# A hybrid trunk kernel: the head by halves, one pool per k tile for u and y, two xbc tiles in one loop, ten conditioning products earlier

## The chip, the cores and the metric

The kernel runs on one core of one Trainium2 chip. Its five engines each take their instructions in order from a queue of their own: TensorE (PE, matrix products, with weight loads shown as PEld), VectorE (DVE), ScalarE (ACT), GpSimd (POOL) and SyncE (SP, here only a queue of transfers). The metric is device time in microseconds (us), lower is better; the median of several executions counts.

## The reference, cut to what matters

One layer over a sequence of 1024 positions with 1024 channels, all in 32-bit floats:

```python
mod = (silu(c) @ w_ada + b_ada).reshape(6, 1024)      # shift1, scale1, gate1, shift2, scale2, gate2
u = rms_norm(x, ln1) * (1.0 + scale1) + shift1
proj = u @ w_in                                       # 1024 -> 11296 columns
gl, cb, cc, cx, z, xbc, dt = split(proj)              # 2048, 3 x 1024, 2048, 4096, 32
y_conv = cb * causal_conv3(cc * cx)
p_conv = y_conv @ w_conv_out
xs, bs, cs = split(silu(causal_conv4(xbc) + bias))    # 2048, 8 x 128, 8 x 128
y = ssd_scan(xs * dt, dt * a, bs, cs) + d_skip * xs   # state-space recurrence, 8 groups
y = group_rms(y * silu(z)) * ssm_norm_w
p_ssm = y @ w_ssm_out
x = x + gate1 * ((sigmoid(gl_a) * p_conv + sigmoid(gl_b) * p_ssm) @ w_o)
u2 = rms_norm(x, ln2) * (1.0 + scale2) + shift2
x = x + gate2 * (square(relu(u2 @ w_up)) @ w_down)
out = rms_norm(x)
```

## The kernel before, in words

Everything is held transposed: channels on the 128 partitions, time along the free axis, in two halves of 512 columns (`hs`). A product of a weight tile with an activation is made with three matmuls, since both are split in a high part and a low part of a faster 32-bit format: high times high, high times low, low times high (`mm3`, L119). One output tile of 128 columns of `w_in` (a *plain* product, `proj`, L126) over 8 k tiles and 2 halves is 48 matmuls of 512 columns; two output tiles are 96. `strassen_pair` (L146) makes two output tiles with 7 block products of 12 matmuls, 84, at the price of sums and differences of weights and results on DVE. It needs combinations of u (`tops_of`, L138, the lists `X`), which are made after the head. Weight tiles come on SP's queue (`wraw`, three buffers), ACT rounds the high part (`whi`), DVE subtracts for the low part (`wlo`), or, in `load_w_acc` (L100), a transfer on POOL's queue adds it up.

The order of work within an engine is chosen by a planner when the program is built: it simulates the engines with a cost model and takes instructions by program order and readiness. `tc.issue_after` pins an instruction behind another. On the chip each engine then follows that fixed order, and waits on semaphores.

*Head* (L267 to L372). `c` is loaded as one row, spread over the partitions by two matmuls, and turned into silu(c) (`cb`). x comes in 16 loads (8 k tiles, 2 halves). ACT squares each, DVE adds the squares, matmuls with a vector of ones sum over partitions (L321), `rsqrt_eps` makes the root for both halves at once, and the diagonal `sdg` times ones spreads it over the partitions (L331). Then a loop over the k tiles j (L342): two conditioning products (`gemv`, L302, a multiply and sum of a 128 x 1024 tile with `cb` on DVE) give the scale and shift columns of this tile; for both halves DVE scales x, ACT adds the shift and rounds (`uh`), DVE makes the residue (`ul`); then PE adds this k tile into four output tiles, f = 0 to 3, both halves, in all eight PSUM banks. The results go through tanh to scratch memory (`gl_d`).

*After the head*: tiles f = 4, 5 are made plain while DVE and ACT make the combinations of u (L380 to L391); the 32 dt columns are projected (L395 to L415, memory in pool `p0d`); then pool `pe1`, which takes over the same bytes, serves the Strassen pairs: f = 6 to 15 (L457), eight pairs for z (L470), twelve for the short convolution (L491). `dt_chain` (L432) is a long run of small DVE operations, placed at f = 8. The other 32 conditioning products (`gemvs`, L423) are placed three per pair from f = 10 on; each loads its tile on POOL's queue into one single buffer, `wv`.

*State-space part* (L547 to L697): for each of eight groups, four xbc tiles are made plain (`xbc_tile`, L560: product, copy to a padded row `raw`, four-tap convolution starting with two ACT operations on PSUM, silu), and the eight chunks of the group before run among them (`ssd_group`). After the last group's tiles, the pool `u` is released (L698), and a pool `yy` on the same side takes over its bytes for the split tiles of y (L700 to L707), which the next products read (`wco`, L713 on; then `wso`, L728 on).

*Rest*, not touched: `w_o`, the second norm, the up and down products and the final norm.

Of the kernel before, what the change touches and what calls it, by code (L numbers as in the profile page):

```python
# [34 lines left out]
NPAR = DSK + 16  # L35


def hybrid_trunk(tc, xT, par, hrows, crow, wada1, wada2, win, wdt, wco, wso, wo, wup, wdt_, wdn, out):
# [20 lines left out]
    prm = cp.tile([P, NPAR], F32, name="prm")  # L59
# [3 lines left out]
    onec = cp.tile([P, P], F32R, name="onec")  # L63
    mcol = cp.tile([P, 48], F32, name="mcol")
    s1c = cp.tile([P, 8], F32, name="s1c")
    s2c = cp.tile([P, 8], F32, name="s2c")
    g1c = cp.tile([P, 8], F32, name="g1c")
    cp.tile([P, 24], F32, name="lpad")
# [193 lines left out]
    p0x = tc.alloc_tile_pool(name="p0x", bufs=1)  # L262
    p0 = tc.alloc_tile_pool(name="p0", bufs=2)
# [7 lines left out]
    crw = glp.tile([1, T], F32, name="crw", tag="glt")  # L271
    sp.dma_start(crw, crow)
    sp.dma_start(prm, par)
    for h in (0, 1):
        ps = mm.tile([P, H], F32, name="mm")
        pe.matmul(ps, lhsT=ones[0:1, :], rhs=crw[:, hs[h]], start=True, stop=True)
        act.activation(ct[:, hs[h]], ps, AF.Tanh, scale=0.5)
        stt(cb[:, hs[h]], ct[:, hs[h]], 1.0, ps, ALU.add, ALU.mult)
# [26 lines left out]
    def warm(n, x_):  # L305
        for _ in range(n):
            pe.matmul(wps, lhsT=ones, rhs=x_, start=True, stop=True)

    warm(4, xt[0][0])
    st = ps0.tile([P, H], F32, name="st")  # L310
    for h in (0, 1):
        acc = None
        for k in range(KT):
            sq = p0.tile([P, H], F32, name="ssq" if k else "sacc", bufs=4 if k else 2)
            act.activation(sq, xt[k][h], AF.Square)
            if k:
                tt(acc, acc, sq, ALU.add)
            else:
                acc = sq
        for j in range(4):  # L320
            pe.matmul(st[:, 4 * h + j:4 * h + j + 1], lhsT=acc[:, j * P:j * P + P], rhs=ones[:, 0:1],  # L321
                      start=h == j == 0, stop=True, skip_group_check=True)
    warm(2, acc)
    r = rsqrt_eps(p0, st[:, 0:8], 1.0 / T, [P, 8], "nst")
    rbs = []
    for h in (0, 1):
        dg = p0.tile([P, 4, P], F32, name="sdg", bufs=1)
        rdy = tt(dg, ident.unsqueeze(1).broadcast_to([P, 4, P]),
                 r[:, 4 * h:4 * h + 4].unsqueeze(2).broadcast_to([P, 4, P]), ALU.mult)
        ps = ps0.tile([P, H], F32, name="st")  # L330
        pe.matmul(ps, lhsT=ones, rhs=dg.rearrange("p j t -> p (j t)"), start=True, stop=True)  # L331
        rb = p0x.tile([P, H], F32, name=f"rb{h}")
        rbc = act.copy(rb, ps)
        rbs.append(rb)

    ws = []
    sps = [[None, None] for _ in range(4)]
    for h in (0, 1):
        for f in range(4):
            pl, nm = (mm, "mm") if f < 2 else (ps0, ("sx", "st")[h])  # L340
            sps[f][h] = pl.tile([P, H], F32, name=nm)
    for j in range(KT):  # L342
        if j > 1:
            load_ada(j)
        if j in (0, 1):
            with tc.issue_after(rdy.ins), (tc.issue_after(rbc.ins) if j else contextlib.nullcontext()):
                for f in range(2):
                    ws.append(load_w(win[2 * j + f], raws[2 * j + f]))
        with tc.issue_after(rdy.ins) if j else contextlib.nullcontext():
            gemv(wa[j, 1], 8 + j)  # L350
            gemv(wa[j, 0], j)
        stt(s1c[:, j:j + 1], mcol[:, 8 + j:9 + j], 1.0, prm[:, LN1 + j:LN1 + j + 1], ALU.add, ALU.mult)
        for h in (0, 1):
            x_ = xt[j][h]
            stt(x_, x_, s1c[:, j:j + 1], rbs[h], ALU.mult, ALU.mult)
            rdy = shift_split(uh[j][h], ul[j][h], x_, mcol[:, j:j + 1])
        if j == 0:
            continue
        for jj in ((0, 1) if j == 1 else (j,)):
            for h in (0, 1):  # L360
                for f in range(4):
                    mm3([sps[f][h]], ws[f][0][:, jj * P:jj * P + P], ws[f][1][:, jj * P:jj * P + P],
                        [uh[jj][h]], [ul[jj][h]], jj == 0, jj == KT - 1)

    def gl_evac(f, ps):
        t = glp.tile([P, T], F32, name="glt")
        for h in (0, 1):
            act.activation(t[:, hs[h]], ps[h], AF.Tanh, scale=0.5)
        act.dma_start(gl_d[f], t)

    for f in range(4):
        gl_evac(f, sps[f])  # L372
# [43 lines left out]

    p0d.release()
# [39 lines left out]
    for f in range(6, 16, 2):  # L457
        ts_ = [glp.tile([P, T], F32, name="glt") for _ in (0, 1)]

        def gl_ev(i, h, src):  # L460
            act.activation(ts_[i][:, hs[h]], src, AF.Tanh, scale=0.5)

        if f == 8:
            dt_chain()
        elif f > 8:
            gemvs(3)
        strassen_pair(pe1, win[f], win[f + 1], X, gl_ev)
        for i in (0, 1):
            act.dma_start(gl_d[f + i], ts_[i])
    for g in range(NG):  # L470
        ts_ = [glp.tile([P, T], F32, name="glt") for _ in (0, 1)]

        def z_ev(i, h, src):
            t = ts_[i][:, hs[h]]
            act.activation(t, src, AF.Tanh, scale=0.5)
            stt(t, t, 1.0, src, ALU.add, ALU.mult)

        gemvs(3)
        strassen_pair(pe1, win[gtile(g) + 4], win[gtile(g) + 5], X, z_ev)
        for i in (0, 1):  # L480
            act.dma_start(z_d[2 * g + i], ts_[i])
# [73 lines left out]
    padded = [p2t.tile([P, T + 3], F32, name=f"raw{i}", bufs=1) for i in (0, 1)]  # L555
# [4 lines left out]
    def xbc_tile(win_i, ci, dst):  # L560
        ps = proj(load_w_acc(win[win_i]), uh, ul)
# [4 lines left out]
        for h in (0, 1):  # L566
            act.activation(a[:, hs[h]], ps[h], AF.Identity, bias=hb[:, ci:ci + 1], scale=hw[:, 4 * ci + 3:4 * ci + 4])  # L567
        for j in (2, 1, 0):
            stt(a, raw[:, j:j + T], hw[:, 4 * ci + j:4 * ci + j + 1], a, ALU.mult, ALU.add)
        act.activation(dst, a, AF.Tanh)  # L570
        stt(dst, dst, 1.0, a, ALU.add, ALU.mult)

    def proj_group(g):
# [7 lines left out]
        xbc_tile(b + 2, 16 + g, bf)  # L581
        xbc_tile(b + 3, 24 + g, cf)
# [145 lines left out]
    for b in range(4):  # L728
        yh, yl = [], []
        for k in range(4):  # L730
# [7 lines left out]
            ys = yy.tile([P, 2, T], F32R, name="ys")  # L738
# [49 lines left out]
    yy.release()  # L788
# [282 lines left out]
```

## Time and profile before

| | |
|---|---|
| runs | 2106.76, 2107.31, 2111.0 us; median 2107.31 |
| profiled execution | 2108.83 us, its span 2107.1 us |
| PE busy | 2070.9 us (98%), 9704 matmul records |
| DVE, ACT, POOL busy | 1482.6 (70%), 962.8 (46%), 177.4 (8%) |
| mean granted TensorE clock | 0.990 |

A busy PE counts overlapping matmuls: one that shows 390 ns is followed by the next after about 0.226 us. A few matmul records are missing. In the rows below "L..." is a line of the kernel before; after "<-" in square brackets stands what ended the idle time of the engine ahead of an instruction.

### The profile page before, as it was taken

The numbers are of one execution on the slowest core, as the hardware profiler recorded it, in microseconds if no ns is written. First come the engines' busy times: TensorE is split into PE (matmuls) and PEld (weight loads), VectorE is DVE, ScalarE is ACT, GpSimd is POOL, SyncE is SP. The second block draws the span as 40 slices with busy tenths as digits, with TensorE's granted clock in tenths as the row PEclk, the third lists the DMA queues.
The fourth block names the chain that finished last, engine by engine and source line by source line (L and its number), as shares of the span: only waits on it lengthen the run. The fifth ranks groups of instructions, "written<-read, shape, count | busy, mean of one in ns | idle before, by whom it ended". The sixth has DMA issues, their size and how long they took to land.

```text
span 2107.1 us, 26132 instructions
## 1 busy us (share of the span) xinstructions
PE 2070.9 (98%) x9704; PEld 1689.8 (80%) x9704; DVE 1482.6 (70%) x2312; ACT 962.8 (46%) x1600; POOL 177.4 (8%) x244
## 2 busy tenths in 40 slices
PE   7999999999999999999999999999999999999997
PEld 4778878888888888887877788888888888888887
DVE  7866788676637778878796848745866665668675
ACT  4433333232246768676564531234544454544432
POOL 0001000000000000000000000012000001232213
PEclk8999999999999999999999999999999999999998
DMA  8226554222265455555366686553144347988932
GB/s 306 79 96 204 188 183 169 80 70 72 78 200 112 122 123 136 140 142 142 93 212 213 212 277 200 166 191 123 61 165 165 151 156 261 309 240 252 281 79 80
DMA packets 138224, 344.09 MB, mean 163 GB/s; under 512 B 12993, under 2 KB 48193, under 8 KB 136562
## 3 DMA queue, kind: packets, MB, share of 16 engines
q1 hardware_dynamic: 98978, 202.76, 30.2%
q0 software_dynamic: 26848, 103.82, 17.3%
q10 hardware_dynamic: 12272, 35.85, 4.3%
q8 instruction: 76, 1.25, 0.2%
q14 instruction: 50, 0.41, 0.1%
HBM read 269.83 MB, written 72.55 MB: 162 GB/s over the span
## 4 chain that ended last, share of the span: by engine, by line
PE 86%; issue 7%; DVE 4%; DMA 2%; POOL 1%; ACT 1%; SPq 0%; DVEq 0%; POOLq 0%; ACTq 0%
PE mm L155 26%; PE mm L124 14%; PE mm L122 14%; PE mm L121 14%; PE mm L965 11%; PE B L615 2%; PE B L620 2%; PE C L637 1%; DMA wv<-in_wada 1%; DVE wada L302 1%; PE A L592 1%; POOL wv L426 1%; DMA x<-in_xT 1%; DVE ul L46 1%; DVE x L46 0%
## 5 line engine op out<-in xcount | busy, mean ns | idle before, releaser
L155 PE MATMUL mm<-t,whi 128*128 128x512 f32 x1136 | 349.8, 390 | 1.6 <-DVE cq L43 1.6
L155 PEld LDWEIGHTS mm<-t,whi 128*128 128x128 f32 x1136 | 212.8, 188 | 47.9 <-DVE cq L43 4.0
L121 PE MATMUL mm<-uh,whi 128*128 128x512 f32 x576 | 228.0, 400 | 3.7 <-ACT uh L114 3.2
L122 PE MATMUL mm<-ul,whi 128*128 128x512 f32 x576 | 229.7, 399 | 0.0
L155 PE MATMUL mm<-t,wlo 128*128 128x512 f32 x568 | 220.4, 389 | 0.0
L965 PE MATMUL mm<-op,whi 128*128 128x512 f32 x672 | 206.9, 389 | 0.1
L124 PE MATMUL mm<-uh,wlo 128*128 128x512 f32 x576 | 185.3, 396 | 1.9 <-DVE wlo L43 1.9
L43 DVE TENSOR_TENSOR wlo<-s,whi 128x1024 fp32r<-128x1024 f32 (+1 forms) x126 | 126.5, 1015 | 66.3 <-ACT whi L160 65.4
L43 DVE TENSOR_TENSOR wlo<-wraw,whi 128x1024 fp32r<-128x1024 f32 (+1 forms) x135 | 144.1, 1068 | 15.3 <-ACT whi L95 8.9
L121 PE MATMUL mm<-ys,whi 128*128 128x512 f32 x384 | 149.3, 396 | 3.7 <-ACT ys L110 3.7
L122 PE MATMUL mm<-ys,whi 128*128 128x512 f32 x384 | 149.7, 396 | 1.1 <-DVE ys L43 1.1
L46 DVE SCALAR_TENSOR_TENSOR cacc<-raw,hw,cacc 128x1024 f32<-128x1024 f32 x96 | 122.7, 1278 | 38.5 <-ACT cacc L567 37.9
L965 PEld LDWEIGHTS mm<-op,whi 128*128 128x128 f32 x672 | 126.0, 188 | 26.7 <-issue 0.5
L160 ACT CAST whi<-wraw 128x1024 fp32r<-128x1024 f32 x78 | 65.3, 837 | 161.5 <-PE mm L155 140.9
L155 PE MATMUL mm<-s,whi 128*128 128x512 f32 x448 | 138.4, 389 | 0.7 <-ACT cu L178 0.7
L609 ACT ACTIVATE seg<-acb,acum 128x128 f32<-128x128 f32 x256 | 81.9, 394 | 110.4 <-PE B L615 104.6
L121 PEld LDWEIGHTS mm<-uh,whi 128*128 128x128 f32 x576 | 108.4, 189 | 28.3 <-ACT uh L114 5.3
L965 PE MATMUL mm<-op,wlo 128*128 128x512 f32 x336 | 130.7, 389 | 0.0
L95 ACT CAST whi<-wraw 128x1024 fp32r<-128x1024 f32 x57 | 59.8, 1052 | 152.8 <-PE mm L122 117.6
L124 PEld LDWEIGHTS mm<-uh,wlo 128*128 128x128 f32 x576 | 108.0, 189 | 24.2 <-DVE wlo L43 2.3
L122 PEld LDWEIGHTS mm<-ul,whi 128*128 128x128 f32 x576 | 109.0, 189 | 21.6 <-issue 0.5
L160 ACT CAST whi<-s 128x1024 fp32r<-128x1024 f32 x78 | 81.8, 1050 | 96.2 <-PE mm L155 95.2
(277 smaller groups left out, 4417.4 us busy)
## 6 DMA issues: line engine op xcount, KB each, us to landing
wraw<-in_win SPq DMA_DIRECT2D x87, 512.0 KB
dr<-in_wdt_ SPq DMA_DIRECT2D x108, 256.0 KB
op_d<-hp POOLq DMA_DIRECT2D x12, 1792.0 KB, 6.2
hr<-op_d POOLq DMA_DIRECT2D x42, 512.0 KB, 5.7
wv<-in_wada POOLq DMA_DIRECT2D x32, 512.0 KB, 3.8
wlo<-in_win POOLq DMA_DIRECT2D x32, 512.0 KB, 7.7
acb<-ac_d SPq DMA_DIRECT2D x64, 256.0 KB
wraw<-in_wup SPq DMA_DIRECT2D x32, 512.0 KB
```

What stands on the lines that cost most here:

```text
L43: return eng.tensor_tensor(out=o, in0=a, in1=b, op=op)
L46: return dve.scalar_tensor_tensor(out=o, in0=a, scalar=s, in1=b, op0=op0, op1=op1)
L95: act.copy(hi, raw)
L121: pe.matmul(o, lhsT=wh, rhs=h_, start=start, stop=False)
L122: pe.matmul(o, lhsT=wh, rhs=l_, start=False, stop=False)
L124: last_mm[0] = pe.matmul(o, lhsT=wl, rhs=h_, start=False, stop=stop)
L155: last_mm[0] = pe.matmul(o, lhsT=l_[:, s_], rhs=r_, start=first and k == j == 0, stop=k == 3 and j == 2, skip_group_check=True)
L160: act.copy(hi, src)
L609: act.activation(seg[:, r, :], acb[:, r, :], AF.Relu, bias=acum[:, c, hd:hd + 1], scale=-1.0)
L615: pe.matmul(Bk[o:o + 64, P * (r // 2):P * (r // 2) + P], lhsT=xd[:, r, :], rhs=seg[:, r, :], start=True, stop=True, skip_group_check=True)
L620: pe.matmul(Bk[:, 256 + P * q:256 + P * q + P], lhsT=state[:, 2 * q:2 * q + 2, :].rearrange("p r k -> p (r k)"), rhs=cf[:, cs], start=True ...
L965: pe.matmul(o, lhsT=l_[:, c_], rhs=t[:, r_, k, :], start=first and k == j == 0, stop=k == 3 and j == 2, skip_group_check=True)
```

## The change

1. **Head by halves.** Only the first half of x is loaded ahead of the weights; its squares, sums, root and spread are made alone. The loop over k tiles then makes only the first half of u, and PE adds it into eight output tiles, f = 0 to 7, each joined as soon as its weights are split. The second half's squares are put into steps 3 to 6, its root into step 7; after the loop the second half of u is made, and f = 4 to 7 and then 0 to 3 get it. So f = 4, 5 move into the head, and f = 6, 7, a Strassen pair before, become plain tiles there. The order on PE, ACT, DVE and SP is pinned, instruction by instruction, to the order written.
2. **First scale column on PE.** `wadak`, a block of `w_ada` laid out for PE, and `c` as columns (`CCOL` in `par`) give the scale of k tile 0 by eight one-column matmuls; the product on DVE for it goes.
3. **Weights in the head.** Tiles 0 to 2 come on SP's queue, 3 to 7 on POOL's; the low parts of 6 and 7 by an accumulating transfer. Conditioning tiles have four buffers, not eight.
4. **Ten conditioning products** are placed at the dt projection, in a pool `p0g` with three buffers between `p0d` and `pe1`; three each stay at f = 12 and 14, two each at the eight z pairs. `dt_chain` moves from f = 8 to f = 10.
5. **Start of the convolution**: one ACT operation of 1024 columns on `raw` instead of two of 512 on PSUM, in all xbc tiles; `raw` is padded to T + 32.
6. **Last two xbc tiles** (B and C of group 7): the k loops of both are interleaved.
7. **One pool per k tile** for u (`u0` to `u7`) and per tile for y (`yy0` to `yy7`).

The core of the diff (left out: pool names and releases, the moved definitions, host arrays):

```diff
+    for k in range(KT):
+        up = tc.alloc_tile_pool(name=f"u{k}", bufs=1, side="right")
+        for n, u_ in (("uh", uh), ("ul", ul)):
+            u_.append([up.tile([P, H], F32R, name=f"{n}{k}{h}") for h in (0, 1)])
...
+    def load_f(f):
+        raws.append(wp.tile([P, T], F32, name="wraw", bufs=3))
+        (sp if f < 3 else pool).dma_start(raws[f], win[f])
...
+    def low_by_dma(f):
+        act.mul(wls[f], raws[f], -1.0)
+        pool.dma_start(wls[f], win[f], accum_op=ALU.add)
...
+    load_x(0)
+    sp.dma_start(wk, wadak)
+    sp.dma_start(wa[0, 0], wada1[0, :, 0])
+    for f in range(3):
+        load_f(f)
+    load_ada(1)
+    load_x(1)
+    load_ada(2)
...
+    sums(0)
+    first_col()
+    high(0)
+    high(1)
+    dg = root(0)
+    stt(mcol[:, 8:9], cps[:, 0:1], 0.5, prm[:, BADA + 8:BADA + 9], ALU.mult, ALU.add)
+    scale_of(0)
+    ps = spread(dg)
+    warm(8)
+    gemv(wa[0, 0], 0)
+    scaled(0, 0, ps)
+    low(0)
+    shift_hi(0, 0)
+    keep_rb(ps)
+    high(2)
+    load_f(3)
+    low(1)
+    load_f(4)
+    for j in range(1, KT):
+        scale_col(j)
+        shift_lo(j - 1, 0)
+        if j == 1:
+            for i in (0, 1, 2):
+                part((0,), (0, 1), 0, (i,))
+            part((0,), (2,), 0, (0, 1))
+        scaled(j, 0)
+        gemv(wa[j, 0], j)
+        if j == 1:
+            load_ada(3)
+            low(2)
+            part((0,), (2,), 0, (2,))
+            load_f(5)
+        if j > 2:
+            for k in {3: (0, 1, 2), 4: (3, 4), 5: (5, 6), 6: (7,), 7: ()}[j]:
+                square(1, k)
+        shift_hi(j, 0)
...
+        if j == 3:
+            load_ada(5)
+            part((2,), range(4), 0)
+            part((2,), (4,), 0, (0, 1))
+            low(4)
+            part((0, 1, 2), (4,), 0, (2,))
+            part((0, 1, 2), (5,), 0, (0, 1))
+            load_f(7)
...
+        if j == 7:
+            dg = root(1)
+            part((6,), range(7), 0)
+            keep_rb(spread(dg))
+    shift_lo(7, 0)
+    part((7,), range(7), 0)
+    part(range(KT), (7,), 0)
+    scaled(0, 1)
     for j in range(KT):
...
+        shift_hi(j, 1)
+        if j < KT - 1:
+            scaled(j + 1, 1)
+        rdy = shift_lo(j, 1)
+        if j < 4:
+            gl_half(2 * j, 0)
+        part((j,), range(4, 8), 1)
+    for f in (0, 2):
+        for f_ in (f, f + 1):
+            part(range(KT), (f_,), 1)
...
-    for f in (4, 5):
-        gl_evac(f, proj(ws[f - 4], uh, ul))
+    def gemvs(n, pl, bufs=1):
+        for _, i in zip(range(n), gem):
+            w_ = pl.tile([P, T + 32], F32, name="wv", bufs=bufs)[:, 0:T]
+            pool.dma_start(w_, wada2[i])
+            gemv(w_, 16 + i)
...
+    p0g = tc.alloc_tile_pool(name="p0g", bufs=1, reuse_waits="tile")
+    gemvs(10, p0g, 3)
...
-    for f in range(6, 16, 2):
+    for f in range(8, 16, 2):
...
-        if f == 8:
+        if f == 10:
             dt_chain()
-        elif f > 8:
-            gemvs(3)
+        elif f > 10:
+            gemvs(3, pe1)
...
-        gemvs(3)
+        gemvs(2, pe1)
...
-        for h in (0, 1):
-            act.activation(a[:, hs[h]], ps[h], AF.Identity, bias=hb[:, ci:ci + 1], scale=hw[:, 4 * ci + 3:4 * ci + 4])
+        act.activation(a, raw[:, 3:3 + T], AF.Identity, bias=hb[:, ci:ci + 1], scale=hw[:, 4 * ci + 3:4 * ci + 4])
...
+        ws = [load_w_acc(win[b + i]) for i in (2, 3)]
+        ps = [[mm.tile([P, H], F32, name="mm") for _ in hs] for _ in ws]
+        for i, k in [(0, k) for k in range(4)] + [(i, k + 4 - 4 * i) for k in range(4) for i in (0, 1)] + [(1, k) for k in range(4, KT)]:
+            c_ = slice(k * P, k * P + P)
+            mm3(ps[i], ws[i][0][:, c_], ws[i][1][:, c_], uh[k], ul[k], k == 0, k == KT - 1)
+            if (i, k) == (0, KT - 1):
+                xbc_evac(ps[0], 16 + g, bf)
+        xbc_evac(ps[1], 24 + g, cf)
...
-    yy = tc.alloc_tile_pool(name="yy", bufs=8, side="right", reuse_waits="tile")
+    yys = [tc.alloc_tile_pool(name=f"yy{f}", bufs=1, side="right", reuse_waits="tile") for f in range(8)]
```

`part(js, fs, h, kinds)` issues, for k tiles `js` and output tiles `fs` of half `h`, the matmuls of the kinds 0 (high times high), 1 (high times low part of u) and 2 (low part of the weight times high).

More of the change, by code (lines that the diff above doesn't have):

```diff
@@ L57, in hybrid_trunk @@
     mm = tc.alloc_tile_pool(name="mm", bufs=4, space=PSUM)
-    prm = cp.tile([P, NPAR], F32, name="prm")
+    s1c, s2c, g1c, cc = [cp.tile([P, 8], F32, name=n) for n in ("s1c", "s2c", "g1c", "cc")]
     ident = cp.tile([P, P], F32, name="ident")
@@ L63, in hybrid_trunk @@
     onec = cp.tile([P, P], F32R, name="onec")
+    prm = cp.tile([P, NPAR], F32, name="prm")
     mcol = cp.tile([P, 48], F32, name="mcol")
[L65 to L68, printed above, removed]
+    ccol = cp.tile([P, 8], F32, name="ccol")
     dcs = cp2.tile([P, 64], F32, name="dc")
@@ new lines, in hybrid_trunk, with first_col, square @@
+    wk = p0w.tile([P, T], F32, name="wk", tag="whx")
+    sp.dma_start(wk, wadak)
+    wa[0, 0] = p0.tile([P, T], F32, name="wada", bufs=4)
+    sp.dma_start(wa[0, 0], wada1[0, :, 0])
[4 more added lines that the diff above has]
+    load_ada(2)
+    def first_col():
+        for k in range(KT):
+            pe.matmul(cps[:, 0:1], lhsT=wk[:, k * P:k * P + P], rhs=ccol[:, k:k + 1], start=k == 0, stop=k == KT - 1)
+    accs = {}
+    def square(h, k):
+        sq = p0.tile([P, H], F32, name="ssq" if k else "sacc", bufs=2 if k else 1)
+        act.activation(sq, xt[k][h], AF.Square)
+        if k:
+            tt(accs[h], accs[h], sq, ALU.add)
+        else:
+            accs[h] = sq
@@ L320, in hybrid_trunk, with scale_of, sums @@
+    def scale_of(j):
+        stt(s1c[:, j:j + 1], mcol[:, 8 + j:9 + j], 1.0, prm[:, LN1 + j:LN1 + j + 1], ALU.add, ALU.mult)
+    st = ps0.tile([P, H], F32, name="st")
+    def sums(h):
         for j in range(4):
-            pe.matmul(st[:, 4 * h + j:4 * h + j + 1], lhsT=acc[:, j * P:j * P + P], rhs=ones[:, 0:1],
+            pe.matmul(st[:, 4 * h + j:4 * h + j + 1], lhsT=accs[h][:, j * P:j * P + P], rhs=ones[:, 0:1],
                       start=h == j == 0, stop=True, skip_group_check=True)
-    warm(2, acc)
@@ L324, in hybrid_trunk, with root @@
[L324 to L329, printed above, removed]
+    def root(h):
+        r = rsqrt_eps(p0, st[:, 4 * h:4 * h + 4], 1.0 / T, [P, 4], "nst")
+        dg = p0.tile([P, 4, P], F32, name="sdg", tag="ssq", bufs=2)
+        tt(dg, ident.unsqueeze(1).broadcast_to([P, 4, P]), r.unsqueeze(2).broadcast_to([P, 4, P]), ALU.mult)
+        return dg
@@ L342, in hybrid_trunk @@
-    for j in range(KT):
[L343 to L372, printed above, removed]
+    def scale_col(j):
+        gemv(wa[j, 1], 8 + j)
+        scale_of(j)
+    def scaled(j, h, rb=None):
+        x_ = xt[j][h]
+        stt(x_, x_, s1c[:, j:j + 1], rbs[h] if rb is None else rb, ALU.mult, ALU.mult)
+    def shift_hi(j, h):
+        act.activation(uh[j][h], xt[j][h], AF.Identity, bias=mcol[:, j:j + 1])
@@ new lines, in shift_lo, with part @@
+    def shift_lo(j, h):
+        return stt(ul[j][h], xt[j][h], mcol[:, j:j + 1], uh[j][h].bitcast(F32), ALU.add, ALU.subtract)
+    sps = {}
+    def part(js, fs, h, kinds=(0, 1, 2)):
+        for f in fs:
+            if (f, h) not in sps:
+                pl, nm = (mm, "mm") if (f < 4) == (h == 0) else (ps0, "sx" if f % 4 < 2 else "st")
+                sps[f, h] = pl.tile([P, H], F32, name=nm)
+        for j in js:
+            for f in fs:
+                for i in kinds:
+                    w_, v_ = ((whs, uh), (whs, ul), (wls, uh))[i]
+                    pe.matmul(sps[f, h], lhsT=w_[f][:, j * P:j * P + P], rhs=v_[j][h], start=j == i == 0,
+                              stop=j == KT - 1 and i == 2, skip_group_check=True)
@@ new lines, in gl_half @@
+    def gl_half(f, h):
+        t = glp.tile([P, T], F32, name="glt")
+        for i in (0, 1):
+            act.activation(t[:, hs[i]], sps[f + i, h], AF.Tanh, scale=0.5)
+            act.dma_start(gl_d[f + i][:, hs[h]], t[:, hs[i]])
+    rbs = []
+    warm(9)
+    act.activation(cc, prm[:, CCOL:CCOL + 8], AF.Tanh, scale=0.5)
+    stt(ccol, cc, 1.0, prm[:, CCOL:CCOL + 8], ALU.add, ALU.mult)
+    cps = mm.tile([P, H], F32, name="mm")
+    for k in range(KT):
+        square(0, k)
+    for h in (0, 1):
+        act.activation(ct[:, hs[h]], rows_c[h], AF.Tanh, scale=0.5)
+        stt(cb[:, hs[h]], ct[:, hs[h]], 1.0, rows_c[h], ALU.add, ALU.mult)
@@ L415, in hybrid_trunk @@
     act.copy(z2, ps[:, :C2])
+    p0g.release()
     p0d.release()
```

149 lines of the change are left out of this document (92 added, 57 removed).

## The prediction

> **What bounds the kernel now.** I read the busy slices of the page first, then TensorE's waits over the whole run, then a table of stretches, and then the timeline of the stretches that stand out.
>
> ```profile
> PE   7999999999999999999999999999999999999997
> PEclk8999999999999999999999999999999999999998
> ```
>
> ```profile
> PE st L321 <- DVE sacc L43: 8.2, 2, 5.9
> PE mm L121 <- ACT ys L110: 3.7, 1, 3.7
> ...
> PE mm L155 <- DVE cq L43: 1.9, 5, 0.7
> PE mm L124 <- DVE wlo L43: 1.9, 1, 1.9
> ```
>
> In the table of stretches the columns are length, then busy time of PE, PEld, DVE, ACT and POOL with instruction counts, granted TensorE clock, DMA share, GB/s.
>
> ```profile
> 0.00:33.00 33.00, 18.51 (x37) 8.19 (x37) 20.84 (x43) 17.95 (x27) 1.09 (x8) 0.81 0.95 353
> 33.00:60.00 27.00, 27.00 (x108) 21.64 (x109) 26.34 (x43) 6.09 (x9) 0.00 (x0) 0.91 0.53 178
> ...
> 80.00:106.00 26.00, 23.61 (x95) 18.38 (x94) 18.91 (x29) 12.62 (x23) 0.00 (x0) 0.93 0.40 147
> ...
> 200.00:350.00 150.00, 147.98 (x647) 120.41 (x645) 117.33 (x173) 46.99 (x67) 12.29 (x24) 1.00 0.58 193
> 350.00:600.00 250.00, 250.00 (x1104) 207.02 (x1103) 170.68 (x222) 79.14 (x95) 3.46 (x12) 1.00 0.26 81
> 600.00:1035.00 435.00, 435.00 (x2323) 351.94 (x2321) 318.34 (x584) 297.47 (x600) 30.68 (x39) 1.00 0.54 136
> ...
> 1063.00:1076.00 13.00, 8.18 (x27) 6.02 (x24) 13.00 (x20) 12.96 (x25) 0.00 (x0) 0.74 0.54 173
> ```
>
> TensorE is the bound almost everywhere: 250.00 of 250 us, 435.00 of 435. From 350 to 600, 1104 matmuls of 512 columns fill 250 us, so one costs 250 / 1104 = 0.226 us of the end. An edit pays only where PE stands idle, runs at half clock, or does work that is not the product. Those places are the head (the 33 us before the first real matmul, and short stalls up to 120 us), 2.0 us between 200 and 350, the seam at 1063 to 1076, and the tail after 2050, which the change does not touch.
>
> **The head.** These rows give the old start, and the pieces from which the new one is built.
>
> ```profile
> 6.00 5.82 PE L307 MATMUL mm<-x,ones 128*128 128x512 f32 x8
> ...
> 8.90 2.69 ACT L315 ACTIVATE ssq<-x 128x512 f32<-128x512 f32 x4 [0.25 <-DMA x<-in_xT]
> ...
> 14.13 1.05 PE L321 MATMUL st<-ones,sacc 128*128 128x1 f32 x8 [2.31 <-DVE sacc L43]
> 22.98 0.17 DVE L49 TENSOR_SCALAR nst<-st 128x8 f32<-128x8 f32 x1 [1.96 <-PE st L321]
> 25.25 0.69 DVE L43 TENSOR_TENSOR sdg<-ident,nst 128x512 f32<-128x512 f32 x1
> 26.35 1.53 PE L331 MATMUL st<-sdg,ones 128*128 128x512 f32 x2
> 32.98 1.22 PE L121 MATMUL mm<-uh,whi 128*128 128x512 f32 x2 [3.19 <-ACT uh L114]
> ```
>
> ```profile
> L302 DVE CUSTOM_DVE_ANT_0 wada<-wada,cb,prm 128x1024 f32<-128x1024 f32 x14 | 17.4, 1279 | 0.0
> ...
> L46 DVE SCALAR_TENSOR_TENSOR ul<-x,mcol,uh 128x512 fp32r<-128x512 f32 x16 | 11.3, 749 | 1.7 <-ACT uh L114 0.8
> L114 ACT ACTIVATE uh<-x,mcol 128x512 fp32r<-128x512 f32 x15 | 10.4, 725 | 30.9 <-DVE x L46 30.9
> L46 DVE SCALAR_TENSOR_TENSOR x<-x,s1c,rb 128x512 f32<-128x512 f32 x14 | 9.9, 748 | 0.2
> ```
>
> ```profile
> L43 DVE TENSOR_TENSOR wlo<-wraw,whi 128x1024 fp32r<-128x1024 f32 (+1 forms) x135 | 144.1, 1068 | 15.3 <-ACT whi L95 8.9
> ```
>
> Old: both halves of x are squared and summed before one root, and the first projection matmul starts at 32.98. New: the first half's squares end where they do now, at 8.90 + 2.69 = 11.59, since that half is still loaded first. Then come the last add 0.69 (as sdg), the sums 1.05, the root with its diagonal (22.98 to 25.94, 2.96), the spread 1.53, the scaling 0.75 and the shift 0.73: 11.59 + 0.69 + 1.05 + 2.96 + 1.53 + 0.75 + 0.73 = 19.3. The first scale column now comes from eight one-column matmuls on PE in the root's shadow, and the first shift product (1.28 on DVE) in the spread's. Eight warming matmuls stand behind the spread in PE's queue. The old ones of 512 columns took 5.82 / 4 = 1.46 each, so one of 128 columns is estimated at 0.36 and eight at 2.9; they begin when the spread ends, at 17.8, and hold PE until 20.7. So the first real matmul comes at 20.7, 12.3 earlier.
>
> From there VectorE paces. Per k tile it did two products, two scalings and two residues: 2 x 1.28 + 4 x 0.75 = 5.6 us. For one half it does two products, one scaling, one residue and, beside it, one weight residue of about 1.1 or two adds of 0.69, again 5.2 to 5.5. It thus gives PE half the operands per k tile, but eight output tiles, not four, now draw on each: 192 matmuls (43.4 us) for seven steps (38 us). PE is short of operands in the first steps, while few weight tiles are split, and has a backlog later. Laying the rows of DVE and ACT end to end in the written order, I get waits of PE of 1.4 (first residue of u), 1.7 (residue of weight tile 2), 1.2 (tile 4) and 0.5 in all others: 4.8. After 46 us PE should not wait again; the second half then needs only 1.5 us of DVE per k tile against 2.7 of PE.
>
> What PE must do is 384 matmuls, 86.9 us (eight tiles as plain products; before, six plain and one Strassen pair of 84). The second half's sums and spread add 1.05 + 1.53 = 2.6. And there is the clock:
>
> ```profile
> 84.36 0.73 PE L124 MATMUL mm<-uh,wlo 128*128 128x512 f32 x2 [1.87 <-DVE wlo L43]
> ...
> 106.08 0.39 PE L155 MATMUL mm<-uh,whi 128*128 128x512 f32 x1
> ...
> 119.53 0.79 PE L155 MATMUL mm<-uh,whi 128*128 128x512 f32 x1 [0.95 <-ACT cu L178]
> ```
>
> ```profile
> 86.00:88.00 2.00, 2.00 (x7) 1.52 (x6) 2.00 (x5) 1.18 (x3) 0.00 (x0) 0.50 0.96 350
> ...
> 120.00:122.00 2.00, 2.00 (x6) 1.52 (x6) 1.82 (x4) 1.40 (x3) 0.00 (x0) 0.50 0.00 0
> ```
>
> After a gap of only 0.95 us, and after one of 1.87, the granted clock was 0.50 for about 3.4 us; eight matmuls then cost twice, 1.6 to 1.8 us lost. The new head has a start and two or three such gaps. Part of the slow time falls into waits, so I charge 4.0, as the old head paid at its own start.
>
> End of the second half: 20.7 + 86.9 + 4.8 + 2.6 + 4.0 = 119.0. Behind it stand the dt matmuls. Before, they lie from 106.08 to 119.53 with 12 matmuls of the pair (2.7) among them, and cost 10.7 plus 1.6 of clock behind the 0.95 wait. So the new head with dt ends at 131.3. Before, the pair's other 72 matmuls follow 119.53: 16.3 + 1.6, so the same work ends at 137.4. **Gain 6.1**; it is 2 if the loads or the clock take 4 more, and 10 if the gaps nearly vanish.
>
> **Covered edits of the head.** Five weight loads go to POOL's queue, which is empty in these stretches now (POOL 0.00 from 33 to 106), and two low parts come by an accumulating transfer. The nearest row, wv, lands 3.6 to 5.6 us after its issue; the step that needs each load is at least one k tile (5.3) later, so I take nothing, and 2 us if one misses. x's second half moves behind about 5.9 MB of other loads in SP's queue (by the sizes of the tiles). At 353 GB/s it is there, 8 MB in all, at 23 us, and the squares that need them are written into step 3, near 33: nothing. The ring of conditioning tiles is four instead of eight, so SP waits on a slot and the next load queues behind it, two steps ahead of use: nothing.
>
> **Ten products moved up.**
>
> ```profile
> 158.44 3.74 DMA wv<-in_wada
> ...
> 163.90 3.85 DMA wv<-in_wada
> ```
>
> ```profile
> DMA to landing us min/median/max: 3.6/3.8/5.6
> ```
>
> ```profile
> DVE s L43 <- PE st L412: 19.2, 1, 19.2
> ```
>
> In the old z stage one buffer serves all 32 products, one per 5.46 us (163.90 - 158.44). DVE stands in its queue behind these transfers, and PE's five waits for cq between 200 and 350 follow; that is the 2.0 idle. With ten products done before and two per pair instead of three, most go: **gain 1.3**, between 0 and 2. Ten products at 1.28 add 12.8 us of DVE to the dt stretch, where DVE had its longest wait (19.2, for PE's last dt matmul). DVE is done with the second half near 81 by the same laying out, and with the seven sums (about 20 us) near 101. Three buffers give 5.46 / 3 = 1.8 per product, so the ten end near 123, ahead of dt's end at 130.
>
> **The seam.**
>
> ```profile
> 1062.12 0.48 PE L124 MATMUL mm<-uh,wlo 128*128 128x512 f32 x1
> ...
> 1067.53 0.73 PE L121 MATMUL mm<-ys,whi 128*128 128x512 f32 x2 [3.70 <-ACT ys L110]
> 1069.38 1.22 PE L122 MATMUL mm<-ys,whi 128*128 128x512 f32 x2 [1.12 <-DVE ys L43]
> ```
>
> ```profile
> 1066.42 2.94 ACT L110 CAST ys<-ccs 128x1024 fp32r<-128x1024 f32 x3
> ```
>
> ```profile
> 1068.12 1.22 DVE L43 TENSOR_TENSOR ys<-ccs,ys 128x1024 fp32r<-128x1024 f32 x1
> ```
>
> The first split of y starts only after the last matmul that reads u, since y's tiles take the bytes of the one pool of u. PE waits 4.8 us (13.00 - 8.18), and then runs at half clock: a mean of 0.74 over 13 us is 6.8 us at 0.50, about 2.8 lost. After the change u's k tile 0 is free once the last tile has read it; in the joint order ten steps of six matmuls follow, 60 x 0.226 = 13.6 us. So the first four splits (0.98 on ACT, 1.22 on DVE each) can be done before the last u matmul, and evacuation of the first tile of the two starts early too. DVE is busy 13.00 of 13 in the seam, so I leave 1.6 of the 7.6 standing: **gain 6.0**, between 2 and 7.6.
>
> **The start of the convolution, joined**: one ACT pass of 1024 in place of two of 512 in each of 32 tiles, off the path where PE is busy 435.00 of 435: nothing; if ACT were late, the wait for both raw copies was there already.
>
> **Sum.** 6.1 + 1.3 + 6.0 = 13.4. The profiled execution took 2108.83 (span 2107.1), 1.5 above the median 2107.31: 2108.8 - 13.4 - 1.5 = 2093.9, so 2094.
>
> **Rivals.**
> 1. The head does not pay: VectorE paces it, PE falls to half clock in each step, and what the earlier start wins is lost in gaps. For it: DVE at 26.34 of 27. Against: at half clock PE closes its gaps by being slow, and recovers (27.00 of 27 from 33 to 60, mean clock 0.91). It costs the 6.1: 2100.
> 2. The seam does not close: the planner still queues the splits of y behind the last evacuations, DVE being full. 2100.
> 3. Both, so that the change does almost nothing: 2106.
> 4. Slower: the ten products come late. Their buffers lie in bytes that the first Strassen pair's scratch takes over, so the pair's first sums and copies wait for the last product. At one product per 5.46, that is, if POOL's queue or the planned order does not overlap the three buffers, ten from about 101 end at 156, not 123, and PE, in order, stands some 26 us behind dt: 2094 + 26 = 2120. It decides from about 2.9 us per product on ((130 - 101) / 10). Against: three slots, and transfers of 3.8 us beside a DMA share of 0.40 or less.
> 5. The clock stays up across the new gaps. For it: PE's waits for cq, up to 0.7 long, left it at 1.00 from 200 to 350. Against: the 0.95 at 119.53 did not. The 4.0 of the head goes: 2090. The Trainium skill ("TensorE: Matmul & The Clock Gate", Part 1) lets the clock fall only after an idle window of about 3.4 us; by that rule none of the new gaps would cost it, and the trace, with its 0.50 behind a gap of 0.95, does not agree.
>
> **How the numbers follow.** Chances: forecast 0.55 (own range 2088 to 2099), rival 1 0.13, rival 2 0.14, rival 3 0.06, rival 4 0.05, rival 5 0.07. The low end takes 10 for the head, 7.6 and 2.0: 2088, with 1 more for what I did not see; the high end takes in rivals 1 and 2 with a little of their own spread. 0.2% is 4.2 us, about what a measurement of this kernel tells from no change. Rivals 1, 2 and 5 stay faster by more than that in nearly all their spread, rival 3 is "same", rival 4 slower.
>
> **What would show it.** Right: first real matmul at 20 to 22; PE waits of about 5 us in the next 25, then none to the end of the head; no wait for ys above 1 us near 1050, clock 1.00 there; no cq waits after 200. Wrong: a first real matmul after 25, PE waiting for a transfer on POOL's queue, PE idle by several us behind dt (rival 4), or 0.50 in most slices up to 60 us (rival 1).

## The result and the profile after

The changed kernel is slower: 2120.76 us median (2119.92 to 2124.69, four runs) beside 2107.84 us of the kernel before (2106.76 to 2111.0, four runs), a ratio of 1.0062 with a 95% interval of 1.0049 to 1.0075. The prediction, 2094 in a range of 2087 to 2104, was wrong in sign. The profiled execution took 2119.92 us, its span is 2118.1.

The busy slices of the page after: the first slice is better (8 for 7), and there is a new dip to 7 in slice 24, which covers 1218 to 1271 us.

```profile
PE   8999999999999999999999979999999999999997
...
PEclk9999999999999999999999989999999999999998
```

TensorE's waits after. The one for ys has gone, and of those for cq 1.3 is left of 1.9; the two longest are new, and both belong to one place:

```profile
PE mm L120 <- DVE s L44: 8.7, 2, 7.6
PE C L834 <- ACT sqh L109: 7.1, 1, 7.1
...
PE sx L401 <- DVE wlx L44: 3.0, 1, 3.0
...
PE mm L401 <- DVE ul L47: 2.1, 1, 2.1
...
PE mm L401 <- ACT whi L312: 1.7, 1, 1.7
PE mm L154 <- DVE cq L44: 1.3, 1, 1.3
```

The table of stretches after, same columns as in the prediction:

```profile
0.00:33.00 33.00, 25.84 (x90) 19.44 (x91) 23.69 (x49) 14.49 (x21) 2.90 (x11) 0.95 0.94 353
...
200.00:350.00 150.00, 148.71 (x655) 122.50 (x654) 115.33 (x167) 50.70 (x72) 8.61 (x17) 1.00 0.49 167
350.00:600.00 250.00, 250.00 (x1106) 207.00 (x1105) 162.63 (x210) 76.11 (x89) 4.29 (x13) 1.00 0.27 84
600.00:1035.00 435.00, 435.00 (x2295) 351.69 (x2293) 311.55 (x564) 288.02 (x551) 29.77 (x38) 1.00 0.53 132
1063.00:1076.00 13.00, 13.00 (x70) 10.80 (x69) 7.14 (x16) 4.05 (x10) 0.00 (x0) 1.00 0.81 277
1220.00:1240.00 20.00, 15.37 (x76) 12.13 (x75) 8.09 (x14) 4.70 (x6) 1.08 (x2) 1.00 0.52 178
1240.00:1260.00 20.00, 9.29 (x25) 6.37 (x26) 8.94 (x20) 2.87 (x5) 0.00 (x0) 0.57 0.44 141
```

Head and seam look as forecast: more work of PE ahead of 33, and 13.00 of 13 at clock 1.00 where it was 8.18 at 0.74. In the kernel before, both 20 us stretches from 1220 on are full; now they hold 15.37 and 9.29. In the timeline of that place (start, length, engine, line, operation):

```profile
1237.71 1.06 ACT L826 ACTIVATE zs<-zs 128x1024 f32<-128x1024 f32 x1 [1.70 <-DMA y_d<-zs]
...
1242.44 0.79 PE L834 MATMUL C<-sqh,onec 128*128 128x512 f32 x1 [7.07 <-ACT sqh L109]
...
1247.72 0.32 SPq L841 DMA_DIRECT2D sq<-ssq_d  x1
1248.10 7.95 SPq L936 DMA_DIRECT2D s<-s_d  x8
...
1252.72 1.87 DVE L44 TENSOR_TENSOR s<-mm,s 128x512 f32<-128x512 f32 x3
```

This is the end of the recurrence: the last group's y is stored, squared (`zs`), split, summed by PE (`finish`), and the sum is stored and loaded again for the last root (`sq`). Behind that load in SP's queue stand the loads of `s` into `slots`, the bytes that the state-space pools give back. PE, in order, first stands before `finish` for its squares, then before the next output product, whose PSUM banks are free only when DVE has added `s`.

Why is there nothing else to do? Counted over the matmuls that read `ys`, up to the last `finish` (after, then before; the number is behind the x, and a few records can be missing):

```profile
1000.00:1242.44 242.44, 151.50 (x624) 1.00 0.60 196
```

```profile
1000.00:1215.70 215.70, 120.80 (x487) 0.98 0.58 185
```

In the changed kernel 624 of the 1152 products of ys stand ahead of it in PE's queue, 487 before. 624 is 384 of the short convolution's output (8 tiles of 48), 192 of the first quarter of the state-space output (8 of 24) and two tiles more: all that can be issued before `s`. The chunks of the state space, which begin earlier, have come late. These are the first chunks (C from xe) of groups 0 and 6, before and then after:

```profile
667.82 0.48 PE L637 MATMUL C<-xe,bt 128*128 128x256 f32 x1
...
1051.91 0.59 PE L637 MATMUL C<-xe,bt 128*128 128x256 f32 x2
```

```profile
662.70 0.48 PE L800 MATMUL C<-xe,bt 128*128 128x256 f32 x1
...
1076.51 0.59 PE L800 MATMUL C<-xe,bt 128*128 128x256 f32 x2
```

5.1 us early at group 0, 24.6 late at group 6. PE was never idle in between (435.00 of 435 up to 1035, and 41.50 of 41.5 from there to 1076.5): it made products of u, and from 1046.36 on products of ys, in place of chunks. Nothing was waited for, so no view of waits shows it; the order in PE's queue is another one.

### The profile page after: what moved, and what is told of

Read it like the earlier page. It is cut to its first block, busy times and chain, and to the rows that moved or that the text cites. A ratio compares the mean times of both kernels' runs of the same rounds, so it can differ in the third digit from the quotient of the medians.

```text
span 2118.1 us, 26251 instructions
## 1 busy us (share of the span) xinstructions
PE 2076.3 (98%) x9760; PEld 1700.5 (80%) x9760; DVE 1472.9 (70%) x2310; ACT 960.5 (45%) x1568; POOL 182.3 (9%) x251
## 4 chain that ended last, share of the span: by engine, by line
PE 82%; issue 7%; DMA 6%; DVE 4%; POOL 1%; ACT 1%; SPq 0%; DVEq 0%; POOLq 0%; ACTq 0%
PE mm L154 29%; PE mm L123 12%; PE mm L120 12%; PE mm L121 12%; PE mm L1131 8%; PE B L778 2%; PE mm L401 2%; PE B L783 1%; DMA yr<-y_d 1%; DMA dr<-in_wdt_ 1%; PE C L800 1%; DMA y_d<-zs 1%; PE A L755 1%; POOL wv L549 1%; DMA wv<-in_wada 1%
## 5 line engine op out<-in xcount | busy, mean ns | idle before, releaser
L154 PE MATMUL mm<-t,whi 128*128 128x512 f32 x1104 | 339.4, 389 | 1.3 <-DVE cq L44 1.3
L154 PEld LDWEIGHTS mm<-t,whi 128*128 128x128 f32 x1104 | 207.1, 188 | 44.8 <-DVE cq L44 2.0
L154 PE MATMUL mm<-t,wlo 128*128 128x512 f32 x552 | 214.1, 389 | 0.0
L121 PE MATMUL mm<-ul,whi 128*128 128x512 f32 x512 | 202.9, 396 | 0.0
L120 PE MATMUL mm<-uh,whi 128*128 128x512 f32 x512 | 202.3, 395 | 0.0
L123 PE MATMUL mm<-uh,wlo 128*128 128x512 f32 x512 | 164.7, 396 | 0.0
L159 ACT CAST whi<-wraw 128x1024 fp32r<-128x1024 f32 x76 | 63.6, 837 | 162.5 <-PE mm L154 144.5
L94 ACT CAST whi<-wraw 128x1024 fp32r<-128x1024 f32 x52 | 54.6, 1050 | 155.4 <-PE mm L121 122.5
L47 DVE SCALAR_TENSOR_TENSOR y<-mm,mcol,y 128x512 f32<-128x512 f32 (+1 forms) x100 | 69.3, 704 | 78.4 <-PE mm L1131 39.5
L123 PE MATMUL mm<-ys,wlo 128*128 128x512 f32 x384 | 123.3, 394 | 0.0
L154 PEld LDWEIGHTS mm<-t,wlo 128*128 128x128 f32 x552 | 103.6, 188 | 21.7
```

The lines of the kernel that those rows point to most:

```text
L47: return dve.scalar_tensor_tensor(out=o, in0=a, scalar=s, in1=b, op0=op0, op1=op1)
L94: act.copy(hi, raw)
L120: pe.matmul(o, lhsT=wh, rhs=h_, start=start, stop=False)
L121: pe.matmul(o, lhsT=wh, rhs=l_, start=False, stop=False)
L123: last_mm[0] = pe.matmul(o, lhsT=wl, rhs=h_, start=False, stop=stop)
L154: last_mm[0] = pe.matmul(o, lhsT=l_[:, s_], rhs=r_, start=first and k == j == 0, stop=k == 3 and j == 2, skip_group_check=True)
```

## The experiments

**Theory A**: the joined start of the convolution, priced at nothing, changes the planner's reckoning; it puts products ahead of chunks, and the recurrence's serial end loses its cover. **Rival B**: the closed seam (pools, interleave) does that. **Rival C**: the joined operation, or the head, costs time where it runs. The table has all runs; "ahead" is the number of ys products ahead of the last `finish`, "idle" is 150 or 100 less PE's busy time in 1050 to 1200 and in 1200 to 1300.

| kernel | ratio to before (95%) | ahead | idle 1050-1200 | idle 1200-1300 |
|---|---|---|---|---|
| before | 1 | 487 | 4.8 | 0 |
| changed | 1.0062 (1.0049 to 1.0075) | 624 | 1.1 | 15.3 |
| two-op start | 0.9981 (0.9972 to 0.9990) | 470 | 6.9 | 0 |
| before, joined start | 1.0042 (1.0028 to 1.0055) | 621 | 1.3 | 11.2 |
| joined, paced | 0.9930 (0.9916 to 0.9944) | 474 | 1.0 | 0 |
| two ops on raw | 0.9965 (0.9951 to 0.9979) | 558 | 0 | 7.4 |
| paced, old seam | 0.9939 (0.9926 to 0.9951) | 474 | 0.6 | 0 |
| paced, old head | 0.9961 (0.9949 to 0.9974) | 474 | 1.4 | 0 |
| two-op, GpSimd | 0.9999 (0.9990 to 1.0009) | 474 | 11.1 | 0.7 |
| banks held | 0.9994 (0.9985 to 1.0004) | 592 | 0 | 8.0 |
| two-op, paced | 0.9931 (0.9917 to 0.9945) | 474 | 0 | 0 |
| before, paced | 0.9981 (0.9969 to 0.9994) | 474 | 4.3 | 0 |
| paced, late finish | 0.9985 (0.9974 to 0.9997) | 576 | 1.7 | 8.0 |
| joined, looser pace | 0.9947 (0.9928 to 0.9965) | 530 | 0 | 0.5 |

**Which edit.** Two-op start: the changed kernel with

```diff
-        act.activation(a, raw[:, 3:3 + T], AF.Identity, bias=..., scale=...)
+        for h in (0, 1):
+            act.activation(a[:, hs[h]], ps[h], AF.Identity, bias=..., scale=...)
```

> The changed kernel with the convolution's start as it was (two ACT operations of 512 on the PSUM banks in every xbc tile instead of one of 1024 on raw); head, interleave, pools and products as changed. Theory A (the joined start lets the planner put products of u, and then of ys, ahead of the state-space chunks, and the recurrence's serial end is laid bare): 2091 to 2099 us, first chunk of the last group before 1145 (1156 in the changed kernel), no wait of PE for sqh or for s over 2 us between 1200 and 1260. Rival B (the closed seam itself, interleave and pools, lets the y products run dry while the recurrence ends): 2116 to 2122, the waits of 7.1 and 7.6 us are still there. Rival C (the tail behind 1800, or the head): 2116 to 2122 without those waits.

Before with the joined start is the reverse of that edit, on the kernel before.

> The kernel before with one thing of the change: the joined start of the convolution. Theory A: it alone lays the recurrence's end bare, so slower: 2118 to 2132 us, PE waits for sqh or s of some 10 us or more between 1190 and 1270. Rival B (the seam's two edits make the loss) and the prediction's price of nothing: 2106 to 2109.

The two-op run took 2106.96 us beside 2110.86: the loss goes, from 1.0062 to 0.9981, and so do both late waits. The joined start alone makes the kernel before 0.42% slower (2119.46), with the same new wait:

```profile
PE mm L121 <- DVE s L43: 10.7, 4, 9.1
```

A stands, B falls as the cause of the loss. But the two-op run is 8 us above the 2091 to 2099 expected: the rest of the change gave 4 us, not 13. Its trace has the chunks at the seam, and PE waits there for an operand of a chunk:

```profile
1067.83 1.19 PE L801 MATMUL C<-xe,bt 128*128 128x256 f32 x2 [5.43 <-DVE xe L44]
```

```profile
1060.00:1070.00 10.00, 3.47 (x20) 2.99 (x21) 10.00 (x18) 10.00 (x19) 0.00 (x0) 0.72 0.58 204
```

DVE and ACT are busy 10.00 of 10, with the ys splits, the convolution of the last tiles and chunks all at once.

**Order or operation.** Joined, paced: the changed kernel with an edge in PE's queue only. Each xbc tile's matmuls stand behind the C matmul of a fixed earlier chunk.

```diff
+    def behind(g, i):
+        k, c = ((-2, 4), (-2, 6), (-1, 0), (-1, 2))[i]
+        at_ = Cs.get((g + k, c))
+        return tc.issue_after(at_.ins) if at_ else contextlib.nullcontext()
...
+        with behind(g, i):
+            ps = proj(w_, uh, ul)
...
-                last = pe.matmul(C, lhsT=bt,
+                last = Cs[g, c] = pe.matmul(C, lhsT=bt,
```

> The changed kernel, joined start and all, with an order edge: the matmuls of tile i of a group's four xbc products are queued on PE behind the C matmul of a fixed chunk of the group one or two earlier (tiles 0 and 1 behind chunks 4 and 6 two groups earlier, 2 and 3 behind chunks 0 and 2 of the group before). Nothing is added or taken out. Theory A (the order is the cause, not what the joined operation costs when it runs): 2088 to 2099 us, the last finish before 1225 (1242 in the changed kernel). Rival C (the joined operation itself holds something back: tanh or the taps come later): 2116 to 2122 or more. If the edges hold PE back too hard, waits of PE in 650 to 1050 would show it (0 now).

Two-op, paced has these edges and the two ACT operations.

> The order edges of the joined and paced run (0.993 of before), with the start as two operations on PSUM: the two kernels stand in nearly the same order on PE and differ in the joined operation alone. If the joined operation is worth nothing where it runs (the prediction's price; the loss came from the order alone): 0.992 to 0.995. If it gives something back when the order is held (less ACT time, earlier banks): 0.995 to 0.999. If it costs something there: under 0.992.

Both came out alike, 0.9930 and 0.9931: held in order, the joined operation is worth 0.0001 +- 0.002, the nothing that it was priced at. So the 0.0081 +- 0.0016 that it costs the changed kernel (1.0062 less 0.9981) comes through the order, as far as that 0.002 can tell. The joined, paced kernel took 2097.08 us, 0.7% below the kernel before; it and the two-op, paced one are the fastest here, and no run tells them apart. Its last `finish` comes at 1201.58 instead of 1242.44. The stretch that was at 9.29:

```profile
1240.00:1260.00 20.00, 20.00 (x90) 16.57 (x89) 14.54 (x16) 6.32 (x6) 0.00 (x0) 1.00 0.84 301
```

**What the planner reacts to.** Joining changes two things: ACT's time per tile, and how soon the PSUM banks are free (after the raw copies). Two ops on raw has ACT's two operations, but reading `raw`, so banks come free early. Banks held has the joined operation, and two one-column copies from the banks behind it:

```diff
+        for h in (0, 1):
+            act.copy(pad[:, h:h + 1], ps[h][:, 0:1])
```

> The changed kernel, but the start is two ACT operations of 512 that read raw instead of one of 1024: the PSUM banks are free as early as in the changed kernel, the ACT operations are as many as before. If the early banks alone make the loss: 2114 to 2121 us. If the ACT time that the joined operation saves in the planner's reckoning does: 2091 to 2099. In the planner's order 558 of the 1152 ys products stand ahead of the last finish (624 in the changed kernel, 470 with the two operations on PSUM), so between the two; 66 products later at 0.22 us is 14 us more cover, and I expect 2095 to 2106.

> The changed kernel with two copies of one column from the PSUM banks on ACT behind the joined operation, so that the banks come free as late as with two operations on PSUM; each copy costs ACT little. If the early banks make the loss: 0.998 of before (as with two operations on PSUM). If the ACT time saved in the planner's reckoning makes it: 1.004 to 1.006 as in the changed kernel. By the order of PE's instructions (592 of the ys products ahead of the last finish; 624 in the changed kernel, 558 with two operations on raw, 494 by 1215 with two on PSUM) I expect a wait of 5 to 12 us there and 0.998 to 1.003.

Each goes only a part of the way from 470 products ahead to 624 (558 and 592) and has half of the idle time (7.4 and 8.0 of 15.3). So both count; how much each, these two runs do not tell cleanly, since the two small copies take ACT time of their own. The 0.0029 between the two is not explained by these 0.6 us. In the profiled executions 2.6 us of it stand already at the first chunk of group 0 (661.6 and 664.2); why is open.

**How much cover the end needs.** Paced, late finish moves only the last `finish` and `rstd(1)`, from the products f = 2 and f = 5 of the first output quarter to behind its last:

```diff
-                if f == 2:
-                    finish(prev, last_mm[0])
-                if f == 5:
-                    rstd(1)
...
+                if f == 7:
+                    finish(prev, last_mm[0])
+                    rstd(1)
```

> The joined and paced run with one thing moved: the last group's sum of squares (finish) and the root behind it are queued behind the last product of the first quarter of the output projection (576 ys products ahead of it) instead of its second one (474 there). Nothing else. Theory A (the recurrence's end needs products to cover it: with few left, PE runs dry on s): PE waits 7 to 12 us for s at 1225 to 1260, and 0.996 to 0.999. Rival (the loss of the changed kernel came from the chunks crowding, not from the cover of the end): no such wait, 0.992 to 0.995.

The looser pace has the numbers (-2, 0), (-2, 2), (-2, 4), (-2, 6) in `behind`.

> The joined start with looser edges: tiles 0 to 3 of a group behind chunks 0, 2, 4, 6 two groups earlier, so that products of u may run a tile or two further ahead (26 of them left at the first chunk of group 6; 28 in the two-operation run, 117 in the paced one) and 530 ys products stand ahead of the last finish. By the series so far (474 and less: no idle; 558: 7.4; 592: 8.0; 624: 15.3 us idle in 1200 to 1300): 2 to 7 us idle there, and at the seam chunks and ys splits meet again, a wait of 2 to 7 us for xe or state. 0.995 to 0.999. If tight pacing is not needed: 0.992 to 0.994.

102 products taken out of the cover cost the paced kernel 0.0055, and the wait is the changed kernel's:

```profile
PE mm L120 <- DVE s L44: 7.9, 1, 7.9
```

The looser pace, with 530 ahead, has 0.5 idle. Over all kernels the idle time in 1200 to 1300 grows with the products ahead: none up to 487 (the 0.7 of the GpSimd run is a wait for `gt`, not for `s`), 0.5 at 530, 7.4 to 8.0 at 558 to 592, 11.2 at 621, 15.3 at 624. I had expected 2 to 7 there, and as much at the seam, where the looser pace was idle for 0: by this run, chunks near the splits are not enough to make the two-op run's wait.

**The other parts of the change.** Paced, old seam undoes the interleave and the pools. Paced, old head is the kernel before with joined start, edges, interleave and pools. Before, paced has the edges alone.

> The run with the order edges (joined start, products paced), with the seam's two edits undone: no interleave of the last two xbc tiles, one pool for u and one for ys. The run with both stood at 0.993 of the kernel before. If the seam's edits are worth the 6.0 us of the prediction: 0.9958 of before (about 2102 beside 2111), with a stretch of 5 us or more without work of PE between the last product of u and the first of ys. If they are worth nothing once the chunks are in step (because the vector engine, not the pools, is what is late there): 0.992 to 0.994, the stretch below 2 us. I hold the first for likelier.

> The kernel before with the joined start, the order edges and the seam's two edits: head and conditioning products as before. Against the run with everything (0.993 of before) it gives what the head and the ten products are worth together. Predicted: 7.4 us, so 0.9965 of before (2103.5 beside 2111). By the traces the first chunk of the state space came 2.6 to 6.2 us earlier in the four kernels with the new head, so 0.9942 to 0.996 by them.

> The kernel before with the order edges and nothing else. If the edges only undo what the joined start did to the order: 0.999 to 1.001. If they also close the seam (the chunks of groups 6 and 7 no longer meet the ys splits on the vector engine), as the run with the old seam (0.9939) suggests, that run less the new head and products (0.0031): 0.9955 to 0.998, with under 2 us of PE idle in 1050 to 1200 (4.8 in the kernel before).

Head and ten products: 0.9961 against 0.9930, 0.0031 +- 0.0019 or 6.5 +- 4 us. The seam's edits: 0.9939 against 0.9930, 0.0009 +- 0.0019 or 2 +- 4 us, so my likelier case there (6.0) was wrong; PE is idle for 0.6 with the old pools, since steps of the chunks (1068.02 to 1070.9) now stand between the last products of u and the first of ys. The edges alone give the kernel before 0.0019 +- 0.0013. They too take away most of its wait for ys (0.4 of 4.8 is left); the 4.3 us of idle time in 1050 to 1200, where I expected under 2, are other waits, 1.3 for an operand of a chunk and this one, at 1086.26, behind the copy of a group's sum:

```profile
PE C L646 <- ACT row L682: 2.5, 1, 2.5
```

**DVE at the seam.** In the two-op kernel the eight low halves of the first ys tiles went to GpSimd:

```diff
-        split(y[:, 0, :], y[:, 1, :], ccs)
+        act.copy(y[:, 0, :], ccs)
+        tt(y[:, 1, :], ccs, y[:, 0, :].bitcast(F32), ALU.subtract, eng=pool)
```

> The run with the two-operation start, but the eight subtractions that make the low halves of the first ys tiles are issued on GpSimd instead of the vector engine (1.22 us each there, 9.8 in all, in 1045 to 1075, where the vector engine has no idle time over 1.2 us and PE waits 5.4 and 1.5 us for its xe and xs). Theory D (the vector engine bounds the seam): these waits go, 1050 to 1200 has 3 us of PE idle or less (6.9 there), and the time is 3 to 7 us less than that run's 0.998 of before: 0.9948 to 0.9967. Rival (the planner's order alone puts the chunks there; or GpSimd is too slow and ys is late): 0.997 to 1.000, with a wait of PE for ys of over 3 us.

It was slower than the two-op run (0.9999 and 0.9981), and the wait for xe grew from 5.4 to 11.1. It tells nothing of Theory D, that DVE bounds the seam, because DVE was not relieved: its own operations grew longer (last section). That DVE's load makes the 5.4 is argued from its 10.00 of 10, not shown.

## Why the prediction was wrong, point by point

- **The start of the convolution** is the step that failed: "off the path where PE is busy 435.00 of 435: nothing". As an operation it was nothing (0.0001 +- 0.002). As an input to the planner it was 1.0062 - 0.9981 = 0.0081, 17 us, more than the 13.4 of all the gains. In the profiled executions of the changed and the two-op kernel, whose spans lie 12.3 us apart, 9.5 of it are idle time of PE in 650 to 1300 (16.4 against 6.9). A full PE says that no wait is removed; it does not say that the same work stays in the same order. The prediction weighed the planner's order only for the ten products and the splits of y, and none of its rivals had the order of chunks and products.
- **Head and ten products**: 7.4 forecast, 5.1 earlier at the first chunk, 6.5 +- 4 in time. Right within that, with its parts somewhat late (forecast in brackets): first real matmul at 22.44 (20.7), waits of 2.1, 1.7 and 3.0, 6.7 in sum, in 25 to 42 (4.8), and the second half of the head ended at 122.7 (119.0). The clock fell twice, to 0.57 and 0.58 on average in 42 to 46 and 26 to 29, so rival 5 did not come; by these means and the 0.86 in 23 to 26 I estimate 6.8 us at 0.50 in all, which cost at most half of that, 3.4 (4.0). From 200 to 350 PE is idle for 1.3 instead of 2.0, a gain of 0.7 (1.3).

```profile
22.44 0.71 PE L401 MATMUL mm<-uh,whi 128*128 128x512 f32 x2
25.22 1.22 PE L401 MATMUL mm<-ul,whi 128*128 128x512 f32 x2 [2.06 <-DVE ul L47]
30.53 0.50 PE L401 MATMUL mm<-uh,whi 128*128 128x512 f32 x1 [1.66 <-ACT whi L312]
...
41.58 1.15 PE L401 MATMUL sx<-uh,wlx 128*128 128x512 f32 x3 [2.99 <-DVE wlx L44]
```

- **The seam** is the term that was mis-sized: 6.0 forecast. The rows came as written (no gap, clock 1.00), but not through these edits alone: the kernel before with the joined start, old pools and no interleave, has only 1.3 idle in 1050 to 1200 too (4.8 before); it shares the changed kernel's order (621 products ahead). With the two-op start and the seam's edits PE is idle for 6.9 there. That is rival 2 in its outcome, but not in its wait, which is for a chunk's operand and not for a split of y. With the order held the edits give 2 +- 4. I priced a wait as if its place had one cause.
- **Rival 4** gave 2120, and that is a coincidence. Its place is not where the time went: the ten products started late (114.86, not 101), took (134.32 - 114.86) / 9 = 2.2 us each, short of its 2.9, and PE waited only 1.08 behind dt, for the pair's first copy.

```profile
114.86 1.28 DVE L322 CUSTOM_DVE_ANT_0 wv<-wv,cb,prm 128x1024 f32<-128x1024 f32 x1 [1.49 <-DMA wv<-in_wada]
...
134.32 1.28 DVE L322 CUSTOM_DVE_ANT_0 wv<-wv,cb,prm 128x1024 f32<-128x1024 f32 x1 [0.80 <-DMA wv<-in_wada]
```

- **Left open**: how the planner's costs turn these two effects into this order was not traced, and the 20.2 us by which the first cast of `op` from `hr` comes earlier in the paced profile (1750.0, 1770.2) are 13.5 us of idle time in 650 to 1300 (2.9, 16.4) and a rest, part of it half clock at 1242 to 1257, that was not taken apart.

## What to carry to other kernels

Where a planner orders the queues from modelled costs, an edit of an operation's length or of a buffer's hold time can move other work even if the operation itself is free: count, in the built queue of the bounding engine, what stands ahead of each serial chain's end, before and after. Where a serial chain needs cover, pin the filling work behind the chain's steps; of the seven kernels with such edges here six were faster than the one before by 0.19 to 0.70%, and the seventh, which took the cover away again, by 0.15%. A full engine without waits can still be doing the wrong work first.

## What the runs showed of the hardware that was not expected

**GpSimd and VectorE hold each other up.** The same scalar-tensor-tensor operation, 128x1024 from SBUF, in the two-op run and then in the run with GpSimd's subtractions, followed by a weight residue (1.22 elsewhere):

```profile
1062.87 1.21 DVE L47 SCALAR_TENSOR_TENSOR xs<-xs,cacc 128x1024 f32<-128x1024 f32 x1
```

```profile
1057.73 3.30 DVE L47 SCALAR_TENSOR_TENSOR xs<-xs,cacc 128x1024 f32<-128x1024 f32 x1
...
1061.28 0.28 DVE L44 TENSOR_TENSOR smk<-A,tri 128x128 f32<-128x128 f32 x1
1061.48 2.83 DVE L47 SCALAR_TENSOR_TENSOR xs<-xs,cacc 128x1024 f32<-128x1024 f32 x1
...
1064.57 3.03 DVE L44 TENSOR_TENSOR wlo<-wraw,whi 128x1024 fp32r<-128x1024 f32 x1
```

```profile
1053.29 6.66 POOL L44 TENSOR_TENSOR ys<-ccs,ys 128x1024 fp32r<-128x1024 f32 x2 [3.72 <-ACT ys L872]
...
1060.51 2.72 POOL L44 TENSOR_TENSOR ys<-ccs,ys 128x1024 fp32r<-128x1024 f32 x1
...
1063.81 2.72 POOL L44 TENSOR_TENSOR ys<-ccs,ys 128x1024 fp32r<-128x1024 f32 x1
```

DVE's operations with two inputs in SBUF take 1.6 to 2.1 us more while a subtraction runs on GpSimd; the one with an input in PSUM (`smk` from A, 0.28) does not. Each of the three ends 1.07 or 1.08 us after the end of a subtraction (1059.95, 1063.23, 1066.53), nearly its whole length when alone. It goes the other way too: the first of the two subtractions from 1053.29 starts while DVE adds two SBUF tiles (`zs`, 1053.02 to 1055.37) and takes 4.33, where the median of the eight is 2.56. The Trainium skill ("SBUF — State Buffer", Summary: rules for kernel authors) says that where VectorE has two SBUF inputs and GpSimd's operation reads SBUF, the second to issue blocks until the first is done; these rows agree. Moving 9.8 us from DVE to GpSimd made the kernel slower by 0.0018 +- 0.0013; that the blocking did it is argued, not shown, since the planner's order is not quite the same either (474 and 470 ahead).

**The clock after a gap.** In the changed kernel the granted clock was 0.50 in 1242 to 1246 and in 1253 to 1257, behind the gaps of 7.07 and 7.60, but 1.00 in 32 to 34 behind the gap of 1.66 at 30.53 and 1.00 in 136 to 138 behind 1.08 at 136.28. In the kernel before it was 0.50 behind 0.95 at the same place in the program, the first copy of the first pair. The length of the last gap alone does not tell which, and the prediction's charge of 4.0 for the head had no firmer ground than that.
